# One layer's modulation sums, query projections and Fourier/gate stage in another order, with VectorE's order written out by hand

## The chip, the core and the metric

The kernel runs on one core of a Trainium2 chip. The core has five engines that work side by side, each through a queue of its own: TensorE (PE, matrix products, with a weight load of its own, PEld), VectorE (DVE), ScalarE (ACT), GpSimd (POOL) and SyncE (SP), which here only issues transfers between the chip's memory and SBUF. Matrix products end in PSUM, whose banks are read out by VectorE or ScalarE before they can be used again. The metric is the device time of one execution, in microseconds (us). The kernel before takes 1128.33 us, the median of three runs from 1126.88 to 1129.64.

## The reference

Two layers act on 1024 latent tokens of width 1024 with 256 context tokens. The work in question lies in layer 0. Cut to what matters:

```python
shift, scale, gate = split(silu(c) @ ada_w[i] + ada_b[i], 3)      # modulation, both layers
h  = rms_norm(x, norm_g) * (1 + scale) + shift                    # (1024, 1024)
hc = the same with c_ctx on the 256 context tokens
proj = h @ w_in                                                   # Fourier | q | k | v | gate
q = rope(rms_norm(q));  k, v = keys and values of context and latent tokens (1280)
o = softmax(q0 k0') v - lam * softmax(q1 k1') v                   # 4 heads of two halves
fo = fftn(u, axes=(tokens, channels of a group), norm="ortho").real   # 4 groups of 128 channels
y = concat([fo, rms_norm(o) * (1 - lam_init)]) * silu(gate part of proj)
x = x + gate * (y @ w_out)                                        # then layer 1, a short convolution
```

All is in float32. On TensorE a float32 product is made of three products of rounded parts: a value is split into `hi`, its rounding, and `lo`, the rest, and `hi*hi + lo*hi + hi*lo` is summed.

## The kernel before, in words

**Projections.** `proj_tok(tt, c)` makes a block of 128 tokens by 512 columns: eight pieces k of the inner dimension, three matmuls each (L284 to L286), 24 in all, into a PSUM bank. c=0 gives the keys, c=1 the values (tt = 0 to 9; the v stage), c=2 the queries (tt = 2 to 9; the query stage), c=3 the input of the Fourier mixer for eight blocks called m, in the order 0, 4, 2, 6, 1, 5, 3, 7, the first three made ahead. Inside a block, jobs are taken between the matmuls: at k = 4, 5 or 6 the transposes of an earlier key or query block (`qk_t`, L345 to L356: PE transposes into `ps_t`, ScalarE rounds to `th`, VectorE makes `tl`, both go to memory), and at k = 7 a column sum (`ada_c`, L583 to L587). Before its transpose a query block is normed and rotated (`qk_norm`, `qk_scaled`, `qk_a`): the square on ScalarE, the sum on VectorE, the power -1/2 on GpSimd (L310, L311), then five steps on VectorE to `od`. The transposes run three query blocks behind.

**Modulation sums.** Eight vectors of 512 (the gates of layer 0 and all six parts of layer 1) are made as sums: `ada_load` brings two pieces of 1 MB (`ada_raw`, three buffers of them), `ada_m` multiplies eight row blocks by the conditioning and adds them into `ada_sum`, four in a call (`half` 0 or 1). With `np_` = n the last n of the four are scaled by ScalarE (L573) and added by GpSimd (L574); the others are one VectorE instruction each (L576, L579). After the second half the sum is on a list, and `ada_step` makes a job of it, the column sum `ps_col`, which PE takes at k = 7 of the next block.

**Fourier and gate.** VectorE forms sums and differences of the eight input blocks (`fa`, `fe`, L691 to L698) and splits four results into the arena (`EO`, L706 to L708). For each of the four groups, `fft_a` multiplies the arena by cosines and sines (`ps_gc`, `ps_gs`), and `fft_b` multiplies that along the channels (`ps_fe`, `ps_fo`); `fee` and `mid` are copies out of PSUM. `gate_half(f, half)` makes 512 columns of the gate path directly, 24 matmuls into `ps_feat`. The other gate columns are made in three pairs g by a scheme of seven products instead of eight (`gate_product(g, p)`, p = 1 to 7), 12 matmuls each, into banks X, Y and Z of the pair (p = 6, 7, 4 use X after p = 1). Their left sides are hi and lo parts of `h` or of its sums: `t3` makes the difference for p = 3 and 7 in place, `tk` and `g_less` those for p = 5, 6 and 4, in `arena0`, `arena1` and `t4`. Their right sides come from `gop`, which combines weights on GpSimd and splits them on ScalarE (L61) and VectorE or GpSimd (L62). Of four pieces of each of these differences, one goes to GpSimd (`GE`). The results (`go`, `sg`) are copied or added out of the banks, and the attention follows, whose first head is loaded into the arena.

**What sets the order.** From the v stage on, PE runs in program order and the order on the other engines comes from a scheduler that works by cost estimates:

```python
    man = tc.manual_schedule(engines={ENG.PE})
    man.__enter__()
```

A buffer of a pool is free again when all readers of its last tile are done; a load into it, or an instruction that writes it, waits for that.

Of the kernel before, what the change touches and what calls it, by code (L numbers as in the profile page):

```python
# [37 lines left out]
def block_kernel(tc, A):  # L38
# [522 lines left out]
    def ada_m(half, np_=0):  # L561

        if half == 0 and adas:
            evs.append((*adas.pop(0), post.tile([P, NB], F32, name="ada_sum", tag="o", bufs=4), alds.pop()))
            if adas:
                alds.append(ada_load(*adas[0]))
# [22 lines left out]
    def ada_step(n):  # L589
        if n % 2 and sums:  # L590
            cols.append(lambda a=sums.pop(): ada_c(*a))
# [6 lines left out]
    for tt in range(NK):  # L598
# [6 lines left out]
        ada_m(tt % 2)  # L605
# [6 lines left out]
    for tt in range(NTC, NK):  # L612
# [4 lines left out]
        ada_step(tt)  # L617
        fins.append(qk_a(proj_tok(tt, 2, (5,)), 0, tt))
        ada_m(tt % 2, 2)
# [35 lines left out]
    ada_step(1)  # L655
    for m in (0, 4, 2):
        qk_b(*fins.pop(0))
        pf.append(proj_tok(NTC + m, 3, (5,)))
    assert not (adas or evs or sums or jobs or cols or fins)
    wnext(2)  # L660
    cls("post", "hc", "ada")

# [16 lines left out]
    fx = opn("fx", "right")  # L679


    for n in range(2):
        eo = []
        for m in (n, n + 2):
            psa = pf.pop(0) if pf else proj_tok(NTC + m, 3)
            a = fx.tile([P, NB], F32, name="fa", bufs=1)
            nc.scalar.copy(out=a, in_=psa)
            psb = pf.pop(0) if pf else proj_tok(NTC + m + 4, 3)
            for i, op in enumerate((ALU.add, ALU.subtract)):
                e = fx.tile([P, NB], F32, name=f"fe{i}", bufs=2)  # L690
                nc.vector.tensor_tensor(out=e, in0=a, in1=psb, op=op)  # L691
                eo.append(e)
        ea, oa, eb, ob = eo
# [12 lines left out]
        for (h, l), u in zip(EO, us):  # L706
            nc.scalar.copy(out=h[:, n, :], in_=u)
            nc.vector.tensor_sub(out=l[:, n, :], in0=u, in1=f32(h[:, n, :]))  # L708
    cls("fx")
# [35 lines left out]
    def fft_b(g, ch, cl, sh, sl, dh, dl):  # L745
# [4 lines left out]
        for pp, a, b, i, n in ((p6, dh, dl, 0, 2), (pe, ch, cl, 0, NB), (po, sh, sl, 2, NB)):  # L750
# [3 lines left out]
            if n == 2:  # L754
                nc.vector.tensor_copy(out=mid, in_=p6[:, 0:2])
        e = fev.tile([P, NB], F32, name="fee", bufs=1)
# [31 lines left out]
    def gate_half(f, half):  # L788
# [7 lines left out]
        gate_out(f, half, ge.tile([P, NB], F32, name="sg", bufs=2), ps)  # L796
# [15 lines left out]
    def gate_product(g, p):  # L812
# [6 lines left out]
        new = lambda: go.tile([P, NB], F32, name="go", bufs=5) if go else ge.tile([P, NB], F32, name="sg", bufs=2)  # L819
# [15 lines left out]
    tk = []  # L835

    def g_diff(t, k, a, b, eng):

        x, y = H[a][k[0]], H[b][k[1]]
        tt = lambda i, j, op: eng.tensor_tensor(out=t, in0=i, in1=f32(j), op=op)  # L840
        tt(f32(x[0]), y[0], ALU.subtract)
        tt(t, x[1], ALU.add)
        tt(t, y[1], ALU.subtract)

    def g_less(k, half, eng):
        x = H[half][k + 4]
        eng.tensor_tensor(out=tk[k], in0=f32(x[0]), in1=tk[k], op=ALU.subtract)
        eng.tensor_tensor(out=tk[k], in0=tk[k], in1=f32(x[1]), op=ALU.add)
# [5 lines left out]
    GE = (nc.vector, nc.vector, nc.vector, nc.gpsimd)  # L854
    def t3():
        for k in range(4):
            u = v0[:, hsl[k % 2]]
            g_diff(u, (k, k + 4), 1, 1, GE[k])
            nc.scalar.copy(out=H[1][k][0], in_=u)
# [774 lines left out]
```

## Time and profile before

| what | value |
|---|---|
| median of 3 runs | 1128.33 us (1126.88 to 1129.64) |
| profiled execution | 1128.21 us |
| its span, first to last instruction | 1126.4 us |
| mean granted clock of TensorE | 0.971 |
| PE busy | 1047.5 us (93%), 5118 matmuls |
| VectorE, GpSimd, ScalarE busy | 759.8, 497.8, 479.8 us |
| chain that ended last | PE 56%, VectorE 15%, ScalarE 4%, GpSimd 4% |

A row of the timeline gives the start in us, the duration, the engine, the line, the operation, the tile written and the tiles read, shape and type, and in brackets how long the engine was idle before and what ended it. A window row gives a stretch, its length, the engine's busy time and number of instructions, the granted clock, the share of the transfer engines and their rate.

### The profile page before, as it was taken

The page shows a single profiled execution, that of the slowest core. Times are in us where ns is not written, and L with a number is a line of the kernel's source. Part 1 is how long each engine was busy: PE and PEld are TensorE (multiplying, and loading weights), DVE is VectorE, ACT ScalarE, POOL GpSimd, SP SyncE. Part 2 cuts the span into 40 slices and gives each one's busy share as a digit, 9 for nine tenths or more (in the row PEclk, how much of TensorE's full clock was granted, in tenths as well). Part 3 has the DMA queues.
Part 4 walks back from the last instruction along what each step waited for, and adds up shares of the span by engine and source line. Part 5 has one row for each costly group of instructions (what it writes and reads, how often), then busy time and mean ns, then how long its engine had stood idle before and what let it go on. Part 6 is the DMA issues. An engine that isn't in the chain of part 4 may idle for free.

```text
span 1126.4 us, 14132 instructions
## 1 busy us (share of the span) xinstructions
PE 1047.5 (93%) x5118; PEld 854.1 (76%) x5118; DVE 759.8 (67%) x1073; ACT 479.8 (43%) x868; POOL 497.8 (44%) x422
## 2 busy tenths in 40 slices
PE   4989899979898989999999998989999999999898
PEld 2657688768786869899988886667888888787576
DVE  4599855883859368888883376996545645579842
ACT  4453213311334357777773363544333333343410
POOL 1256002740466325766666446473435343433331
PEclk9998899989898999999999999999999999999899
DMA  9724895533220596451102652022121211211421
GB/s 342 302 96 120 260 292 174 175 102 110 73 99 10 142 263 142 126 133 60 48 29 95 226 166 94 1 76 74 43 70 38 68 45 56 74 56 64 160 86 65
DMA packets 61381, 131.12 MB, mean 116 GB/s; under 512 B 5248, under 2 KB 30208, under 8 KB 58112
## 3 DMA queue, kind: packets, MB, share of 16 engines
q1 hardware_dynamic: 60240, 125.64, 35.6%
q0 software_dynamic: 1072, 4.59, 1.1%
q8 instruction: 40, 0.66, 0.3%
q14 instruction: 29, 0.24, 0.1%
HBM read 105.57 MB, written 24.64 MB: 116 GB/s over the span
## 4 chain that ended last, share of the span: by engine, by line
PE 56%; DVE 15%; ACT 4%; POOL 4%; issue 3%; DMA 0%; ACTq 0%; DVEq 0%; POOLq 0%
PE psX L649 6%; PE psX L650 6%; PE psX L651 6%; PE ps_av L1032 5%; PE psY L650 3%; PE psY L651 3%; PE psY L649 3%; PE S L982 3%; PE S L983 3%; PE ps_t L1022 2%; DVE nm L987 2%; PE ps_feat L1085 2%; PE ps_feat L1087 2%; PE ps_feat L1086 2%; PE psZ L651 1%
## 5 line engine op out<-in xcount | busy, mean ns | idle before, releaser
L61 ACT CAST wop<-wraw 128x512 fp32r<-128x512 f32 x152 | 93.2, 620 | 129.3 <-PE psY L651 28.4
L62 POOL TENSOR_TENSOR wop<-wraw,wop 128x512 fp32r<-128x512 f32 x72 | 100.7, 1402 | 71.2 <-ACT wop L61 71.2
L284 PE MATMUL ps_tok<-whi,hhi 128*128 128x512 f32 x288 | 120.8, 420 | 2.4 <-ACT hhi L393 2.4
L285 PE MATMUL ps_tok<-whi,hlo 128*128 128x512 f32 x288 | 117.6, 408 | 3.8 <-DVE hlo L397 3.8
L286 PE MATMUL ps_tok<-wlo,hhi 128*128 128x512 f32 x288 | 116.4, 404 | 0.0
L987 DVE TENSOR_REDUCE nm<-S 128x1 f32<-128x1280 f32 x64 | 95.0, 1487 | 21.7 <-PE S L983 18.7
L649 PE MATMUL psX<-B,wop 128*128 128x512 f32 x240 | 98.3, 410 | 11.6 <-DVE out L1363 3.4
L998 ACT ACTIVATE p<-S,nm 128x1280 f32<-128x1280 f32 x64 | 85.2, 1331 | 44.1 <-DVE nm L987 38.3
L650 PE MATMUL psX<-B,wop 128*128 128x512 f32 x240 | 97.8, 408 | 1.6 <-POOL B L1454 1.0
L651 PE MATMUL psX<-B,wop 128*128 128x512 f32 x240 | 97.3, 405 | 0.5 <-POOL wop L62 0.5
L628 POOL TENSOR_TENSOR s<-wraw 128x512 f32<-128x512 f32 x20 | 27.4, 1370 | 125.6 <-DMA wraw<-in_wodd_dram 118.5
L62 DVE TENSOR_TENSOR wop<-wraw,wop 128x512 fp32r<-128x512 f32 x80 | 65.6, 823 | 20.4 <-ACT wop L61 20.1
L1032 PE MATMUL ps_av<-v,aT 128*128 128x128 f32 x640 | 76.8, 275 | 0.0
L628 POOL TENSOR_TENSOR wraw<-wraw 128x512 f32<-128x512 f32 x40 | 56.4, 1420 | 43.0 <-DVE wop L62 35.5
L1032 PEld LDWEIGHTS ps_av<-v,aT 128*128 128x128 f32 x640 | 74.2, 192 | 0.2
L285 PEld LDWEIGHTS ps_tok<-whi,hlo 128*128 128x128 f32 x288 | 56.7, 197 | 18.8 <-DVE hlo L397 7.5
L284 PEld LDWEIGHTS ps_tok<-whi,hhi 128*128 128x128 f32 x288 | 56.7, 197 | 16.9 <-ACT hhi L393 3.7
L1009 POOL TENSOR_TENSOR p<-p,cc 128x256 f32<-128x256 f32 x32 | 40.3, 1261 | 65.2 <-DVE cc L1006 46.1
L649 PEld LDWEIGHTS psX<-B,wop 128*128 128x128 f32 x240 | 46.4, 193 | 26.8 <-issue 5.7
L650 PE MATMUL psY<-B,wop 128*128 128x512 f32 x160 | 63.8, 399 | 2.8 <-DVE B L1216 2.4
L286 PEld LDWEIGHTS ps_tok<-wlo,hhi 128*128 128x128 f32 x288 | 56.6, 197 | 12.3
L651 PE MATMUL psY<-B,wop 128*128 128x512 f32 x160 | 63.5, 397 | 1.5 <-DVE wop L62 1.5
(344 smaller groups left out, 2683.8 us busy)
## 6 DMA issues: line engine op xcount, KB each, us to landing
ada_raw<-in_ada_dram SPq DMA_DIRECT2D x24, 1024.0 KB, 6.8
wraw<-in_wodd_dram SPq DMA_DIRECT2D x32, 512.0 KB, 3.5
wraw<-in_wo_dram SPq DMA_DIRECT2D x24, 512.0 KB, 4.6
wraw<-in_wtok_dram SPq DMA_DIRECT2D x16, 512.0 KB, 5.0
arena<-kd SPq DMA_DIRECT2D x16, 320.0 KB, 8.8
kq<-kd SPq DMA_DIRECT2D x16, 320.0 KB, 9.8
xt<-in_xT_dram SPq DMA_DIRECT2D x16, 256.0 KB, 5.9
xr<-in_xT_dram SPq DMA_DIRECT2D x16, 256.0 KB, 4.0
```

What stands on the lines that cost most here:

```text
L61: nc.scalar.copy(out=o[:, 0, :], in_=src)
L62: eng.tensor_tensor(out=o[:, 1, :], in0=src, in1=f32(o[:, 0, :]), op=ALU.subtract)
L284: nc.tensor.matmul(ps, lhsT=hh, rhs=whi, start=k == 0, stop=False)
L285: nc.tensor.matmul(ps, lhsT=hl, rhs=whi, start=False, stop=False)
L286: nc.tensor.matmul(ps, lhsT=hh, rhs=wlo, start=False, stop=k == KT - 1)
L628: tt = lambda out, x, y, op: nc.gpsimd.tensor_tensor(out=out, in0=x, in1=y, op=op)
L649: nc.tensor.matmul(ps, lhsT=a, rhs=x[k][0], start=start and k == 0, stop=False, skip_group_check=not start)
L650: nc.tensor.matmul(ps, lhsT=a, rhs=x[k][1], start=False, stop=False, skip_group_check=not start)
L651: nc.tensor.matmul(ps, lhsT=b, rhs=x[k][0], start=False, stop=k == 3, skip_group_check=not start)
L987: nc.vector.tensor_reduce(out=nm, in_=S[m][:, :NKEY], op=ALU.max, axis=AX.X, negate=True)
L998: nc.scalar.activation(out=p, in_=S[m][:, :NKEY], func=AF.Exp, bias=tiles.pop((i, m, "nm")), accum_out=z)
L1032: nc.tensor.matmul(ps, lhsT=groups[i, k // 4][:, (k % 4) * P:(k % 4 + 1) * P], rhs=v[:, k * P:(k + 1) * P], start=k == 0, stop=k == NK - 1)
```

## The change

The sums. They are held in three kinds of buffers (`o`, `gt1_1`, `gt2_1`) instead of one. The v stage starts them at tt = 1 instead of 0, and takes half (tt+1)%2. A column sum is now only made a job while another sum is on the list (or no load is left), the oldest first, so that it comes a block pair later: the first four moved from blocks 3, 5, 7, 9 of the v stage to 5, 7, 9 and query block 4, the others from query blocks 3, 5, 7, 9 to 6, 8 and m = 0 and 2. In the query stage a half is wholly on ScalarE and GpSimd when tt is even, wholly on VectorE when it is odd; before, each half was shared two and two.

Fourier and gate. From there on VectorE, too, runs in program order. `tk` is formed early: two pieces between projections, two after the first half of the arena. All pieces that GpSimd had of `t3`, `tk` and `t4` go to VectorE. `t3` is in two parts around the first `fft_a`. Two gate halves stand before the first `fft_a`, and the rounding by ScalarE and the rest on VectorE are one step apart (`lagged`). `mid` is copied by ScalarE, `fee` lies in `v0`, `sg` has three buffers. The products come in another order, and a product's matmuls stand ahead of the next weight combination. The number of PE instructions is the same.

On PE, in the v stage (a piece of the difference; `ps_tok` is a projection, `ps_col` a column sum):

```order
 L285 MATMUL ps_tok<-whi,hlo 128x512
 L286 MATMUL ps_tok<-wlo,hhi 128x512
-L586 MATMUL ps_col<-ones,ada_sum 128x1 x4
 L284 MATMUL ps_tok<-whi,hhi 128x512
 L285 MATMUL ps_tok<-whi,hlo 128x512
```

The first column sum no longer stands in block 3; nothing takes its place there.

On GpSimd, in the second half of the query stage (`s` is the norm of a query block, one number behind it for each block). Before:

```order
L310 TENSOR_SCALAR s_1743<-s_1743 128x8
L574 TENSOR_TENSOR ada_sum<-ada_sum,ada_raw 128x512
L311 TENSOR_TENSOR s_1743<-s_1743,mhalf 128x8
L310 TENSOR_SCALAR s_1806<-s_1806 128x8
L311 TENSOR_TENSOR s_1806<-s_1806,mhalf 128x8
L574 TENSOR_TENSOR ada_sum<-ada_sum,ada_raw 128x512 x2
L310 TENSOR_SCALAR s_1862<-s_1862 128x8
L311 TENSOR_TENSOR s_1862<-s_1862,mhalf 128x8
L574 TENSOR_TENSOR ada_sum<-ada_sum,ada_raw 128x512 x2
```

And now:

```order
L310 TENSOR_SCALAR s_1789<-s_1789 128x8
L575 TENSOR_TENSOR ada_sum<-ada_sum,ada_raw 128x512
L311 TENSOR_TENSOR s_1789<-s_1789,mhalf 128x8
L575 TENSOR_TENSOR ada_sum<-ada_sum,ada_raw 128x512 x3
L310 TENSOR_SCALAR s_1852<-s_1852 128x8
L575 TENSOR_TENSOR ada_sum<-ada_sum,ada_raw 128x512
L311 TENSOR_TENSOR s_1852<-s_1852,mhalf 128x8
L575 TENSOR_TENSOR ada_sum<-ada_sum,ada_raw 128x512
L310 TENSOR_SCALAR s_1910<-s_1910 128x8
L311 TENSOR_TENSOR s_1910<-s_1910,mhalf 128x8
```

Four adds stand between two norms where two stood, and none behind the last norm.

On VectorE, between the last Fourier input block and the first FFT (`fe` are sums and differences of input blocks, `gop` gate weights, `arena` what the FFT reads, `v` a work tile). Before:

```order
L691 TENSOR_TENSOR fe_2244<-fa,ps_tok 128x512
L695 TENSOR_TENSOR v_2066<-fe_2186,fe_2242 128x512
L695 TENSOR_TENSOR v_2066<-fe_2188,fe_2244 128x512
L695 TENSOR_TENSOR fe_2186<-fe_2186,fe_2242 128x512
L62 TENSOR_TENSOR gop<-graw,gop 128x512
L695 TENSOR_TENSOR fe_2188<-fe_2188,fe_2244 128x512
L62 TENSOR_TENSOR gop<-s_2478,gop 128x512
L708 TENSOR_TENSOR arena_2064<-v_2066,arena_2064 128x512
L708 TENSOR_TENSOR arena_2065<-v_2066,arena_2065 128x512
L708 TENSOR_TENSOR arena_2064<-fe_2186,arena_2064 128x512
L62 TENSOR_TENSOR gop<-graw,gop 128x512
L708 TENSOR_TENSOR arena_2065<-fe_2188,arena_2065 128x512
```

And now:

```order
L708 TENSOR_TENSOR fe_2259<-v_2073,ps_tok 128x512
L708 TENSOR_TENSOR fe_2261<-v_2073,ps_tok 128x512
L715 TENSOR_TENSOR v_2073<-fe_2198,fe_2259 128x512
L715 TENSOR_TENSOR fe_2198<-fe_2198,fe_2259 128x512
L715 TENSOR_TENSOR v_2073<-fe_2200,fe_2261 128x512
L715 TENSOR_TENSOR fe_2200<-fe_2200,fe_2261 128x512
L728 TENSOR_TENSOR arena_2071<-v_2073,arena_2071 128x512
L728 TENSOR_TENSOR arena_2071<-fe_2198,arena_2071 128x512
L728 TENSOR_TENSOR arena_2072<-v_2073,arena_2072 128x512
L728 TENSOR_TENSOR arena_2072<-fe_2200,arena_2072 128x512
```

The three `gop` rows that stood among the arena's pieces are gone from there, and the arena comes in one piece (L728 is L708 of before).

The diff, cut to its core:

```diff
         if half == 0 and adas:
-            evs.append((*adas.pop(0), post.tile([P, NB], F32, name="ada_sum", tag="o", bufs=4), alds.pop()))
+            tag, n = (("o", 4), ("gt1_1", 1), ("gt2_1", 1))[len(adas) % 3 - 2]
+            evs.append((*adas.pop(0), post.tile([P, NB], F32, name="ada_sum", tag=tag, bufs=n), alds.pop()))
             if adas:
...
     def ada_step(n):
-        if n % 2 and sums:
-            cols.append(lambda a=sums.pop(): ada_c(*a))
+        if n % 2 and sums and (len(sums) > 1 or not adas):
+            cols.append(lambda a=sums.pop(0): ada_c(*a))
...
         ps = proj_tok(tt, 1, (4,))
-        ada_m(tt % 2)
+        if tt:
+            ada_m((tt + 1) % 2)
         v = post.tile([P, NB], F32, name="vo", tag="o", bufs=4)
...
             qk_b(*fins.pop(0))
-        ada_step(tt)
+        ada_step(tt + 1)
         fins.append(qk_a(proj_tok(tt, 2, (5,)), 0, tt))
-        ada_m(tt % 2, 2)
+        ada_m((tt + 1) % 2, 4 * (tt % 2 == 0))
     wnext(3)
...
     pf = []
-    ada_step(1)
     for m in (0, 4, 2):
         qk_b(*fins.pop(0))
+        ada_step((0, 4, 2).index(m) + 1)
         pf.append(proj_tok(NTC + m, 3, (5,)))
     cls("post", "hc", "ada")
+    man.__exit__(None, None, None)
+    man = tc.manual_schedule(engines={ENG.PE, ENG.DVE})
+    man.__enter__()
...
     fx = opn("fx", "right")
+    tk = []
+    for i in range(2):
+        tk += halves(wp.tile([P, T], F32, name="tk", tag="wraw", bufs=2))
+
+    def g_diff(t, k, a, b):
+
+        x, y = H[a][k[0]], H[b][k[1]]
+        tt = lambda i, j, op: nc.vector.tensor_tensor(out=t, in0=i, in1=f32(j), op=op)
+        tt(f32(x[0]), y[0], ALU.subtract)
+        tt(t, x[1], ALU.add)
+        tt(t, y[1], ALU.subtract)
+
             psa = pf.pop(0) if pf else proj_tok(NTC + m, 3)
-            a = fx.tile([P, NB], F32, name="fa", bufs=1)
+            a = v0[:, NB:T]
             nc.scalar.copy(out=a, in_=psa)
                 eo.append(e)
+            if m == 1:
+                g_diff(tk[2], (2, 2), 1, 0)
+                g_diff(tk[3], (3, 3), 1, 0)
         ea, oa, eb, ob = eo
...
             nc.vector.tensor_sub(out=l[:, n, :], in0=u, in1=f32(h[:, n, :]))
+        if n == 0:
+            g_diff(tk[0], (0, 0), 1, 0)
+            g_diff(tk[1], (1, 1), 1, 0)
     cls("fx")
...
             if n == 2:
-                nc.vector.tensor_copy(out=mid, in_=p6[:, 0:2])
-        e = fev.tile([P, NB], F32, name="fee", bufs=1)
+                nc.scalar.copy(out=mid, in_=p6[:, 0:2])
+        e = v0[:, 0:NB]
         nc.scalar.copy(out=e, in_=pe)
...
             nc.tensor.matmul(ps, lhsT=b, rhs=H[half][k][0], start=False, stop=k == KT - 1)
-        gate_out(f, half, ge.tile([P, NB], F32, name="sg", bufs=2), ps)
+        gate_out(f, half, ge.tile([P, NB], F32, name="sg", bufs=3), ps)
...
-    tk = []
-
-    def g_diff(t, k, a, b, eng):
-
-        x, y = H[a][k[0]], H[b][k[1]]
-        tt = lambda i, j, op: eng.tensor_tensor(out=t, in0=i, in1=f32(j), op=op)
-        tt(f32(x[0]), y[0], ALU.subtract)
-        tt(t, x[1], ALU.add)
-        tt(t, y[1], ALU.subtract)
-
-    def g_less(k, half, eng):
+    def g_less(k, half):
         x = H[half][k + 4]
-        eng.tensor_tensor(out=tk[k], in0=f32(x[0]), in1=tk[k], op=ALU.subtract)
-        eng.tensor_tensor(out=tk[k], in0=tk[k], in1=f32(x[1]), op=ALU.add)
+        nc.vector.tensor_tensor(out=tk[k], in0=f32(x[0]), in1=tk[k], op=ALU.subtract)
+        nc.vector.tensor_tensor(out=tk[k], in0=tk[k], in1=f32(x[1]), op=ALU.add)
     GB = {1: H[0][:4], 2: H[0][4:], 3: H[1][4:], 7: H[1][:4]}
-    GE = (nc.vector, nc.vector, nc.vector, nc.gpsimd)
-    def t3():
-        for k in range(4):
-            u = v0[:, hsl[k % 2]]
-            g_diff(u, (k, k + 4), 1, 1, GE[k])
-            nc.scalar.copy(out=H[1][k][0], in_=u)
-            GE[k].tensor_tensor(out=H[1][k][1], in0=u, in1=f32(H[1][k][0]), op=ALU.subtract)
+
+    def lagged(steps):
+
+        held = None
+        for a, b in steps:
+            r = a()
+            if held:
+                held()
+            held = lambda b=b, r=r: b(r)
+        held()
+
+    def rounded(src, hi):
+        nc.scalar.copy(out=hi, in_=src)
+
+    def rest(src, hi, lo):
+        nc.vector.tensor_tensor(out=lo, in0=src, in1=f32(hi), op=ALU.subtract)
+
+    def t3(ks):
+        def a(k):
+            u = ge.tile([P, NB], F32, name="s1", bufs=1) if k % 2 else v0[:, NB:T]
+            g_diff(u, (k, k + 4), 1, 1)
+            rounded(u, H[1][k][0])
+            return u
+
+        lagged([(lambda k=k: a(k), lambda u, k=k: rest(u, *H[1][k])) for k in ks])
+
+    def tpart(q, ks, half=None):
+
+        def a(k):
+            if half is not None:
+                g_less(k, half)
+            rounded(tk[k], q[k][:, 0, :])
+
+        lagged([(lambda k=k: a(k), lambda _, k=k: rest(tk[k], q[k][:, 0, :], q[k][:, 1, :])) for k in ks])
     gload(1)
-    for i in range(2):
-        tk += halves(wp.tile([P, T], F32, name="tk", tag="wraw", bufs=2))
-    for k in range(4):
-        g_diff(tk[k], (k, k), 1, 0, GE[k])
     gate_half(0, 1)
+    gate_half(1, 1)
+    t3((0, 1))
     cur = fft_a(0)
-    for g, fh in ((1, (1, 1)), (2, (0, 0)), (3, (1, 0))):
-        gate_half(*fh)
-        fft_b(*cur)
-        cur = fft_a(g)
-        if g == 1:
-            t3()
-            gop(0, 1)
-            gop(1, 1)
-            gop(0, 5)
+    t3((2, 3))
+    gate_half(0, 0)
+    gop(0, 1)
+    gop(1, 1)
+    fft_b(*cur)
+    cur = fft_a(1)
+    gate_half(1, 0)
+    gop(0, 5)
+    gop(0, 2)
+    fft_b(*cur)
+    cur = fft_a(2)
     gate_product(0, 1)
+    gop(1, 5)
+    fft_b(*cur)
+    cur = fft_a(3)
     gate_product(1, 1)
+    gop(1, 2)
+    qs = [quarter_of(t) for t in arena]
+    tpart(qs[0], range(4))
     fft_b(*cur)
     t4 = go.tile([P, 8 * NB], F32R, name="t4")
-    qs = [quarter_of(t) for t in (*arena, t4)]
-    GB.update({5: [(q[:, 0, :], q[:, 1, :]) for q in qs[0]], 6: [(q[:, 0, :], q[:, 1, :]) for q in qs[1]],
-               4: [(q[:, 0, :], q[:, 1, :]) for q in qs[2]]})
-    for k in range(4):
-        part(tk[k], qs[0][k], GE[k])
-    gop(0, 6)
-    for k in range(4):
-        g_less(k, 1, GE[k])
-        part(tk[k], qs[1][k], GE[k])
-    gop(0, 2)
-    gop(0, 7)
-    gop(1, 5)
-    for k in range(4):
-        g_less(k, 0, GE[k])
-        part(tk[k], qs[2][k], GE[k])
-    order = [(0, 5), (0, 6), (0, 2), (0, 7), (1, 5), (0, 4), (1, 6), (0, 3), (1, 7), (1, 2),
-             (2, 1), (1, 4), (2, 5), (2, 6), (1, 3), (2, 7), (2, 2), (2, 4), (2, 3)]
-    ahead = order[5:]
+    qs.append(quarter_of(t4))
+    for p, q in zip((5, 6, 4), qs):
+        GB[p] = [(t[:, 0, :], t[:, 1, :]) for t in q]
+    tpart(qs[1], range(4), 1)
+    order = [(0, 5), (0, 2), (1, 5), (1, 2), (0, 6), (1, 6), (0, 7), (1, 7), (0, 4), (0, 3), (1, 4), (1, 3),
+             (2, 1), (2, 5), (2, 6), (2, 2), (2, 7), (2, 4), (2, 3)]
+    ahead = order[4:]
     for n, (g, p) in enumerate(order):
+        gate_product(g, p)
+        if n in (2, 3):
+            tpart(qs[2], (2 * n - 4, 2 * n - 3), 0)
         if ahead:
                 gload(q[0] + 2)
-        gate_product(g, p)
     nc.scalar.activation(out=l2[:, 0:1], in_=last[0][:, 0:1], func=AF.Exp)
```

More of the change, by code (lines that the diff above doesn't have):

```diff
@@ L818, in gate_product @@
         f = 2 + 2 * g
-        new = lambda: go.tile([P, NB], F32, name="go", bufs=5) if go else ge.tile([P, NB], F32, name="sg", bufs=2)
+        new = lambda: go.tile([P, NB], F32, name="go", bufs=5) if go else ge.tile([P, NB], F32, name="sg", bufs=3)
         if p in (1, 6):
```

## The prediction

> **What bounds the kernel now.** I read the busy times first, then the waits of TensorE, then its timeline around each wait, and last the timelines of the engines named there.
>
> ```profile
> PE 1047.5 (93%) x5118; PEld 854.1 (76%) x5118; DVE 759.8 (67%) x1073; ACT 479.8 (43%) x868; POOL 497.8 (44%) x422
> ```
>
> TensorE (PE) is busy 93% of the span and each other engine 67% at most, so time goes where PE stops or runs slowly. Every wait of PE from 120 to 400 us (line waited at, what released it, us in total, times, longest):
>
> ```profile
> PE ps_col L586 <- POOL ada_sum L574: 8.0, 2, 6.7
> PE ps_col L586 <- DVE ada_sum L576: 4.7, 1, 4.7
> PE ps_gc L732 <- DVE arena L708: 3.9, 2, 3.5
> PE ps_fo L751 <- ACT fee L757: 3.3, 1, 3.3
> PE psX L649 <- ACT go L822: 2.2, 1, 2.2
> ```
>
> These 22.1 us lie at places that the diff touches. A stop costs more than its length, as PE's timeline shows (start, duration, instruction, what it waited for):
>
> ```profile
> 129.72 0.40 PE L286 MATMUL ps_tok<-wlo,hhi 128*128 128x512 f32 x1
> 134.79 1.84 PE L586 MATMUL ps_col<-ones,ada_sum 128*128 128x1 f32 x8 [4.68 <-DVE ada_sum L576]
> 142.80 0.60 PE L349 MATMUL ps_t<-cst,od 128*128 128x128 f32 x4
> ...
> 150.98 0.40 PE L286 MATMUL ps_tok<-wlo,hhi 128*128 128x512 f32 x1
> 152.02 0.48 PE L284 MATMUL ps_tok<-whi,hhi 128*128 128x512 f32 x1
> ...
> 212.80 0.40 PE L286 MATMUL ps_tok<-wlo,hhi 128*128 128x512 f32 x1
> 215.44 0.47 PE L284 MATMUL ps_tok<-whi,hhi 128*128 128x512 f32 x1
> ...
> 227.15 0.40 PE L286 MATMUL ps_tok<-wlo,hhi 128*128 128x512 f32 x1
> 242.75 0.60 PE L349 MATMUL ps_t<-cst,od 128*128 128x128 f32 x4
> 243.43 0.39 PE L285 MATMUL ps_tok<-whi,hlo 128*128 128x512 f32 x1
> 248.41 0.39 PE L286 MATMUL ps_tok<-wlo,hhi 128*128 128x512 f32 x1
> 248.64 0.60 PE L349 MATMUL ps_t<-cst,od 128*128 128x128 f32 x4
> ```
>
> Undisturbed, 22 matmuls lie between 243.43 and 248.41, so one takes 0.226 us; a block of 24 with its transposes takes 248.64 - 242.75 = 5.89; and a matmul with the column sum behind it takes 152.02 - 150.98 = 1.04, 0.09 more with the slower start after it. I call the five places A to F, with B and C for the two stops in the first row. A: 129.72 to 142.80 is 13.08 for a column sum and 15 matmuls, which need 1.04 + 0.09 + 15 x 0.226 = 4.52; lost 8.56. B: 215.44 - 212.80 - 1.04 = 1.60. C: 242.75 - 227.15 = 15.60, with 18 matmuls, so 15.60 - 1.13 - 4.07 = 10.40. What A and C lose beyond their stops (8.56 - 4.68 = 3.88 and 10.40 - 6.7 = 3.70) is the clock (window, busy, granted clock, DMA):
>
> ```profile
> 230.00:232.00 2.00, 0.00 (x0) 0.81 0.58 115
> 234.00:236.00 2.00, 1.74 (x9) 0.50 0.93 310
> 240.00:242.00 2.00, 2.00 (x7) 0.63 0.00 0
> ```
>
> It falls during the stop, and PE, back at work, is at half speed from 234 until about 241. The gate stage's three:
>
> ```profile
> 289.73 0.28 PE L730 MATMUL ps_gc<-tabs,arena 128*128 128x256 f32 x1
> 299.96 0.39 PE L793 MATMUL ps_feat<-hhi,whi 128*128 128x512 f32 x1
> 307.16 0.28 PE L730 MATMUL ps_gc<-tabs,arena 128*128 128x256 f32 x1
> 310.67 0.40 PE L793 MATMUL ps_feat<-hhi,whi 128*128 128x512 f32 x1
> ...
> 338.31 0.40 PE L753 MATMUL ps_fe<-gcl,cht 128*128 128x512 f32 x1
> 347.29 0.40 PE L649 MATMUL psY<-arena,gop 128*128 128x512 f32 x1
> ...
> 355.88 0.50 PE L649 MATMUL psX<-hhi,gop 128*128 128x512 f32 x1 [2.16 <-ACT go L822]
> ```
>
> D: the first fft_a takes 10.23, the second 3.51; lost 6.72. E: 338.31 to 347.29 is 8.98 for 13 matmuls, which need 13 x 0.226 + 0.09 = 3.03; lost 5.95. F: the stop itself, 2.16. A to C are 20.56, D to F 14.83, together 35.39, of which the slow clock is 3.88 + 3.70 + (6.72 - 3.92) + (5.95 - 3.30) = 13.0. The sum is made against the profiled execution, 1128.21 us, 0.12 below the median of 1128.33. With all six gone it would be 1092.8, which bounds the gain, since PE's work is the same.
>
> [...]
>
> **A to C, the modulation sums.** The eight sums keep their work; the column sums of the first four come two blocks later (first now in block 5 of the v stage), those of the last four later as well, the eighth in m=2 of the Fourier input instead of query block 9. A's sum had been released at 134.79; its new place is two blocks behind 129.72, at 129.72 + 2 x 24 x 0.226 = 140.6. Lead 5.8 us, cost 0. C's sum ended on GpSimd:
>
> ```profile
> 228.15 1.97 POOL L311 TENSOR_TENSOR s<-s,mhalf 128x8 f32<-128x8 f32 x1
> 230.55 3.65 POOL L574 TENSOR_TENSOR ada_sum<-ada_sum,ada_raw 128x512 f32<-128x512 f32 x2 [0.43 <-issue]
> ```
>
> It would now be read 3 x 5.89 = 17.7 us later. B likewise. So 20.56 us go, unless something that stood behind the adds becomes late. In the even query blocks all four adds are on GpSimd (4 x 3.65 / 2 = 7.3 us in a block of 5.89), none in the odd ones, so over two blocks with two norms (2.0 each) it has 11.3 us of work against 11.8: tight, but the transposes that need the norm run three blocks behind. Tighter is m=4, whose transpose waits for VectorE's `tl`, and this stands in VectorE's queue behind weight splits for which ScalarE first does the four scalings of the eighth sum:
>
> ```profile
> ada_raw<-in_ada_dram SPq DMA_DIRECT2D x24, 1024.0 KB, 6.8
> ...
> 215.16 1.34 ACT L573 ACTIVATE ada_raw<-ada_raw,cs 128x512 f32<-128x512 f32 x2 [6.56 <-DMA ada_raw<-in_ada_dram]
> 233.93 1.04 ACT L171 CAST whi<-wraw 128x1024 fp32r<-128x1024 f32 x1 [7.15 <-DMA wraw<-in_wg_dram]
> ...
> 235.13 1.22 DVE L172 TENSOR_TENSOR wlo<-wraw,whi 128x1024 fp32r<-128x1024 f32 x1
> 338.53 0.67 DVE L847 TENSOR_TENSOR tk<-hhi,tk 128x512 f32<-128x512 f32 x1
> ```
>
> The chain: load 6.8, scalings 2 x 1.34, casts 3 x 1.04, subtractions 3 x 1.22, a weight load (half the size of the sums' pieces, so above 3.4; estimated 4), `tl` 0.67: 20.9 us. In the order it starts 3.6 blocks ahead of PE's need, 21.2 us. Without lead, four hops that each wait for one instruction of 0.67 make it 2.7 late. Below: 0. Above: twice that with E's clock loss, 5.4 + 2.65 = 8.0. I take 2.7, the four hops.
>
> **D, the first FFT.** Two gate halves (48 x 0.226 = 10.8 us of PE) now stand ahead of it instead of one. VectorE has ten instructions of 0.67 between the eighth projection and the last arena piece, and no gate weights between them: 6.7 us plus one ScalarE cast of about 0.6, 7.3 against 10.8. D goes whole. If the cover is gone (the second gate half waits for its weights), D's 6.72 stays.
>
> **E, the odd half of fft_b.** It waited for the copy of `fee`, last in ScalarE's queue behind this:
>
> ```profile
> 339.84 0.62 ACT L61 CAST arena<-tk 128x512 fp32r<-128x512 f32 x1 [0.26 <-DVE tk L848]
> 341.36 0.59 ACT L757 COPY fee<-ps_fe 128x512 f32<-128x512 f32 x1
> ```
>
> Now the casts ahead of the last fft_b round `tk` that VectorE finished long ago, and what needs VectorE comes behind. ScalarE takes over the copy of `mid`, bounded by 0 and a full copy's 0.59; 0.4, nearer to the copy since the cost of starting stays. In the third fft_b the `fee` copy may stand behind a gate cast of 0.62: between 0 and 0.7, 0.35.
>
> **F, the product order.** The X bank alternates between groups, so the wait at 355.88 goes. Two costs: (0,6) comes fifth and needs the new arena1 pieces from VectorE, by my walk 0.7 early to 1.3 late, bounded 0 to 1.5, taken 0.75. And (2,7) to (2,4) share a bank back to back: PE waits for the matmul's drain, 0.17 more than its pitch (0.39 - 0.226), and a ScalarE copy, 0.59 as that of `fee`: 0.8. All that PE has left stands behind each of these two waits. VectorE takes 14 instructions from GpSimd, 12 pieces of `tk` move ahead of the first FFT; hidden while VectorE has idle time, and it has:
>
> ```profile
> 284.00:400.00 116.00, 75.87 (x94) 0.94 0.29 85
> 340.00:360.00 20.00, 19.63 (x21) 0.83 0.00 0
> ```
>
> 75.9 busy of 116, so 40.1 idle, though little of it in the second row. Price if the cover is gone: 14 x 0.67 = 9.4, at most 14 x 1.77 = 24.8 by this row beside GpSimd's work:
>
> ```profile
> 333.93 1.77 DVE L847 TENSOR_TENSOR tk<-hhi,tk 128x512 f32<-128x512 f32 x1
> ```
>
> **Sum.** 1128.21 - 35.39 + 2.7 + 0.4 + 0.35 + 0.75 + 0.8 = 1097.8, 1098 us.
>
> **The rivals.** First: the query stage stays late. The four adds in one piece push the norm or the weight splits past m=0 and m=4, with a stop at each and the halved clock. Priced between E (5.95) and C (10.40), 8.2 each, in place of the 2.7: 1097.8 - 2.7 + 16.4 = 1112. For it: 11.3 us of work in 11.8 on GpSimd. Against: three blocks of lead.
>
> Second: VectorE in program order is late at (0,6). Twelve VectorE instructions make the arena1 pieces, behind four for arena0; if half of the sixteen run at 1.77 instead of 0.67, (0,6) stops 8.8 us, with E's clock loss 2.65: 1097.8 + 11.4 = 1109. For it: 19.63 busy of 20 in 340 to 360. Against: four products (4 x 12 x 0.226 = 10.8 us) now stand ahead of it, and GpSimd has fewer instructions to disturb it. [...]
>
> Third: the sums' loads land late in the new buffers and A to C stay while D to F go: 1097.8 + 20.6 - 2.7 = 1116. For it: DMA is busy 0.93 at 234 to 236. Against: in program order a load moves by at most one block, its column sum by two or more.
>
> Fourth, slower: VectorE's idle time is no cover. In program order it waits at the head of its queue for PE's banks and ScalarE's casts, its 40.1 us stay idle as they were, and the 14 moved instructions come on top of the gate stage at 1.77: 1128.2 - 20.56 + 24.8 = 1132, D to F giving nothing. It is slower from 13 of the 14 exposed (23.0 against 20.56 + 2.3) and no change for 11 or 12. For it: an order by hand does not pass a waiting instruction. Against: the `tk` part lies where VectorE has only the Fourier sums to do.
>
> **How the numbers follow.** The likeliest 0.62 with 1098, its own range 1092.8 to 1092.8 + 8.0 + 0.6 + 0.7 + 1.5 + 0.8 = 1104; first 0.16, second 0.11, third 0.03, fourth 0.08 (half of it within 0.2%). A measurement tells 0.2%, 2.3 us, from no change. All but the fourth are faster: 0.92; same 0.04; slower 0.04. The range of 1092 to 1113 holds the likeliest and the first two, leaving out the third and fourth and the upper tails.
>
> **What would show it.** Right: no wait of `ps_col` for the sums, none of `ps_gc` for the arena, the granted clock at 1.00 from 126 us on, the Fourier input's last projection some 20 us earlier than 284. Wrong: a wait of `ps_t` or `ps_tok` over 3 us between 215 and 250 (first), a `psX` wait for arena at the fifth product (second), `ps_col` still waiting (third), VectorE over 90% busy through the gate stage with PE waiting for `gop` (fourth). A time over 1113 would mean that a new stop with its own halved clock has come.

## The result and the profile after

The changed kernel takes 1100.43 us (median of four runs, 1098.48 to 1103.36) against 1128.99 for the kernel before (four runs); the ratio is 0.9749, interval 0.9729 to 0.9769. Forecast were 1098 us and a range of 1092 to 1113. The profiled execution of the changed kernel is the slowest of its four, 1103.36 us with a span of 1101.6. TensorE's waits from 100 to 400 us (line waited at, what released it, us in total, times, longest):

```profile
...
PE ps_t L349 <- DVE tl L353: 2.3, 1, 2.3
PE psX L653 <- DVE gop L62: 2.2, 1, 2.2
...
PE psX L651 <- ACT go L852: 0.7, 1, 0.7
...
PE ps_fo L774 <- ACT mid L778: 0.3, 1, 0.3
PE ps_col L587 <- DVE tl L353: 0.2, 1, 0.2
```

None of the five waits of before is left: no `ps_col` for a sum, no `ps_gc` for the arena, no `ps_fo` for `fee`, and the two `psX` waits are others. The rows left out are the attention's. In the order of size the new ones are the transpose of m=4, the product (0,6), the reuse of the X bank by (2,4), and the copy of `mid`: the four places that the prediction named. TensorE's timeline around the first two (start, duration, instruction, in brackets the wait):

```profile
227.49 0.39 PE L286 MATMUL ps_tok<-wlo,hhi 128*128 128x512 f32 x1
230.20 1.11 PE L349 MATMUL ps_t<-cst,od 128*128 128x128 f32 x4 [2.32 <-DVE tl L353]
237.50 0.39 PE L286 MATMUL ps_tok<-wlo,hhi 128*128 128x512 f32 x1
...
328.46 0.40 PE L652 MATMUL psX<-arena,gop 128*128 128x512 f32 x1
331.07 0.50 PE L653 MATMUL psX<-arena,gop 128*128 128x512 f32 x1 [2.21 <-DVE gop L62]
335.97 0.40 PE L652 MATMUL psX<-arena,gop 128*128 128x512 f32 x1
```

From 227.49 to 237.50 is one block, 10.01 us instead of 5.89: 4.1 lost. From 328.46 to 335.97 there are 15 matmuls of 0.23, 3.45 us, in 7.51: 4.1 lost. About half of each is the clock (window, length, busy time and matmuls, granted clock, transfer share, rate):

```profile
230.00:231.00 1.00, 0.80 (x5) 0.58 0.62 180
...
233.00:234.00 1.00, 1.00 (x5) 0.71 0.82 229
...
332.00:333.00 1.00, 1.00 (x6) 0.78 0.00 0
...
335.00:336.00 1.00, 1.00 (x4) 0.51 0.62 238
```

The clock of a window tells when in it the speed changed: 0.58 is half speed for (1 - 0.58) x 2 = 0.84 us, so it fell at 230.16, as the stop ended (at 230.20). At the second place it fell at 332.56, 1.5 us after TensorE had gone back to work at 331.07.

The sum over the stages: 35.39 us of losses are gone, 4.1 + 4.1 + 0.7 + 0.3 = 9.2 are new, which makes 26.2. The first score product of the attention started at 401.18 and now starts at 375.76, 25.4 earlier, although this execution was 1.2 us late before the change begins (85.46 before, 86.68 after, the same instruction of the key stage), so 26.6 by the trace. The medians lie 28.6 apart; the other 2 us stand in no trace here. The two instructions, first before, then after:

```profile
85.46 0.79 PE L285 MATMUL ps_tok<-whi,hlo 128*128 128x512 f32 x1 [0.63 <-DVE hlo L397]
401.18 0.50 PE L982 MATMUL S<-arena 128*128 128x512 f32 x1 [0.78 <-DVE go L825]
```

```profile
86.68 0.50 PE L285 MATMUL ps_tok<-whi,hlo 128*128 128x512 f32 x1 [0.74 <-DVE hlo L397]
375.76 0.47 PE L1019 MATMUL S<-arena 128*128 128x512 f32 x1 [0.83 <-issue]
```

### The profile page after: what moved, and what is told of

The parts are those of the page before. It is cut to its first block, busy times and chain, and to the rows that moved or that the text cites. A ratio compares the mean times of both kernels' runs of the same rounds, so it can differ in the third digit from the quotient of the medians.

```text
span 1101.6 us, 14113 instructions
## 1 busy us (share of the span) xinstructions
PE 1037.6 (94%) x5118; PEld 846.6 (77%) x5118; DVE 756.2 (69%) x1079; ACT 481.7 (44%) x876; POOL 484.6 (44%) x412
## 4 chain that ended last, share of the span: by engine, by line
PE 64%; DVE 20%; POOL 5%; issue 5%; ACT 5%; DMA 0%; ACTq 0%; POOLq 0%; DVEq 0%
PE psX L651 6%; PE psX L653 6%; PE psX L652 6%; PE ps_av L1069 5%; PE ps_tok L284 3%; PE ps_tok L285 3%; PE ps_tok L286 3%; PE psY L652 3%; PE psY L653 3%; PE psY L651 3%; PE S L1019 3%; PE S L1020 3%; DVE nm L1024 2%; PE ps_t L1059 2%; PE ps_feat L1122 2%
## 5 line engine op out<-in xcount | busy, mean ns | idle before, releaser
L285 PE MATMUL ps_tok<-whi,hlo 128*128 128x512 f32 x288 | 115.2, 400 | 3.8 <-DVE hlo L397 3.8
```

The costliest lines, as they stand in the source:

```text
L285: nc.tensor.matmul(ps, lhsT=hl, rhs=whi, start=False, stop=False)
```

## The experiments

Theory: each of the losses A to F went at its own place, for the reason that the prediction gave, and the two stops that are left are VectorE's order. Rivals: the parts depend on each other; the gain comes from VectorE's program order as such; GpSimd is what matters. Ratios are against the kernel before, timed alongside.

| edit | median us | ratio, interval |
|---|---|---|
| the change | 1100.43 | 0.9749, 0.9729 to 0.9769 |
| e1 sums only | 1118.68 | 0.9905, 0.9869 to 0.9940 |
| e2 gate stage only | 1114.20 | 0.9870, 0.9833 to 0.9907 |
| e3 VectorE scheduled | 1101.54 | 0.9760, 0.9728 to 0.9791 |
| e4 one gate half ahead | 1099.24 | 0.9738, 0.9708 to 0.9768 |
| e5 weights of (0,6) ahead | 1098.75 | 0.9747, 0.9726 to 0.9768 |
| e6 eighth sum shared | 1100.70 | 0.9761, 0.9734 to 0.9788 |
| e7 all halves shared | 1101.57 | 0.9770, 0.9756 to 0.9785 |
| e8 e5 and e6 | 1099.38 | 0.9753, 0.9739 to 0.9767 |
| e9 late weight splits | 1098.36 | 0.9744, 0.9719 to 0.9768 |
| e10 e3 and e4 | 1100.27 | 0.9760, 0.9738 to 0.9782 |
| e11 a quarter on GpSimd | 1103.50 | 0.9791, 0.9766 to 0.9817 |
| e12 e9 and e5 | 1098.15 | 0.9737, 0.9714 to 0.9760 |

From e3 on the times lie within half a per cent of one another, and their intervals overlap, but for e11 and e12. What tells these apart is the trace, by the waits.

**e1: the sums alone.** The kernel before with this part of the diff:

```diff
-        ada_m(tt % 2)
+        if tt:
+            ada_m((tt + 1) % 2)
...
-        ada_m(tt % 2, 2)
+        ada_m((tt + 1) % 2, 4 * (tt % 2 == 0))
...
+        ada_step((0, 4, 2).index(m) + 1)
```

with the buffers and `ada_step` as in the change.

> The kernel before with the change of the modulation sums alone; Fourier and gate stage as before. Theory (the terms of the prediction add up, each at its place): A to C vanish (20.56 us) and the transpose of m=4 stops as in the changed kernel, where 227.49 to 237.50 took 10.01 us instead of 5.89, so 4.1 with its slow clock; gain 16.4, some 1112 us. D, E and F stay, with the waits of ps_gc, ps_fo and psX at 3.9, 3.3 and 2.2 us. Rival (the parts are tied: the scheduler's order of VectorE spoils the query stage without the program order behind it): ps_col or ps_t still waits over 4 us, gain under 10, over 1118 us.

The gain was 9.5 us (1128.14 to 1118.68), not 16.4. The rival held: `ps_t` waits 6.3 us. The sums no longer stop TensorE, and the waits of D, E and F are as before, but `ps_t` stops twice instead of once, and the first is longer. Waits, then VectorE's timeline:

```profile
PE ps_t L349 <- DVE tl L353: 3.4, 1, 3.4
PE ps_t L349 <- DVE od L340: 2.9, 1, 2.9
```

```profile
230.57 3.07 DVE L842 TENSOR_TENSOR tk<-tk,hlo 128x512 f32<-128x512 f32 x2
...
238.94 0.68 DVE L340 TENSOR_TENSOR od<-ko,kn 128x512 f32<-128x512 f32 x1
```

The scheduler, with VectorE free of order, draws the gate stage's `tk` into the query stage, ahead of the last `od`; two more of its pieces (1.28 us from 226.43) stand ahead of the late `tl`. In the change `tk` stands behind the Fourier sums by program order.

**e2: the gate stage alone.** The changed kernel with the sums as before (the edits of e1 reversed).

> The changed kernel with the modulation sums as before; Fourier and gate stage as changed. Theory: D to F (14.83 us) are gone, and the new stops of the changed kernel come in their place: 4.1 at (0,6) with its slow clock, 0.9 at (2,4), 0.3 in fft_b; net gain 9.5, some 1119 us, with ps_col waiting 4.7 and 8.0 us as before. Rival (the gate stage gains only because the sums are out of the way earlier): gain under 5, over 1123 us. Gains of this and of the sums alone should add up to the whole, 28.6.

Gain 13.9 us, more than the theory's 9.5 and near the whole of D to F. `ps_col` waits 4.5 and 8.5 us as before, (0,6) stops 2.2 again, up to 346.10, but in the profiled execution the clock did not fall after it (1.00 in every window of 1 us from 346 to 358). The gains of e1 and e2 sum to 23.4 against 28.6; by their intervals (6.8 to 14.8, and 10.5 to 18.8) the times do not refute that they add up, while the trace names what e1 alone pays: the stop of 2.9 us, half speed from 239.4 to 242.8 behind it, and a `tl` stop of 3.4 instead of 2.3. That E and F go with the gate stage's edits as a whole is shown here; which of these edits removes each was not tried.

**e3: VectorE's order from the scheduler.**

```diff
-    man = tc.manual_schedule(engines={ENG.PE, ENG.DVE})
+    man = tc.manual_schedule(engines={ENG.PE})
```

> The changed kernel with VectorE's order from the scheduler again, all else as changed. Theory (the gain of D to F comes from the cover ahead of the first FFT and from the product order, not from VectorE's program order): within 3 us of the changed kernel, 1098 to 1104; no ps_gc wait over 1 us although two gop rows again stand among the arena's. Rival (program order itself is what removes D and E): ps_gc or ps_fo waits over 2 us again and the time is 1105 to 1112.

The theory held: no wait of `ps_gc`, `mid` at 0.8, and (0,6) does not stop at all. It pays elsewhere: `ps_t` at m=4 now waits 3.4 for `tl`, with pieces of `tk` ahead of it in VectorE's queue, as in e1, and half speed from 229.2 to 236.0.

**e4: one gate half ahead.**

```diff
-    gate_half(1, 1)
-    t3((0, 1))
     cur = fft_a(0)
+    gate_half(1, 1)
+    t3((0, 1))
```

> The changed kernel with one gate half instead of two ahead of the first FFT, the other behind it, as it was before; VectorE in program order. Theory (the cover of D is the second gate half): in the changed kernel the last arena piece ended 7.9 us after the eighth projection, one gate half lasts 5.4, and the FFT's first pieces are needed at once, so ps_gc waits 1 to 2.5 us, with one slow stretch of the clock of 0 to 1.7: 1101 to 1105. Rival (the program order alone, without gop rows among the arena's, removes D): ps_gc waits under 0.5, within 1 us of the changed kernel.

The rival held: with half of the cover the FFT stops 0.2 us. The second gate half is not what removes D.

```profile
PE ps_gc L755 <- DVE arena L728: 0.2, 1, 0.2
```

**e10: both of these undone.** The edits of e3 and e4 together.

> The changed kernel with both undone: one gate half instead of two ahead of the first FFT, and VectorE's order from the scheduler. Either alone left no stop at the FFT. Theory (D's stop had two causes, each of which alone is enough to remove it: gop rows among the arena's pieces, and too little cover): with both back ps_gc waits 1.5 to 4 us and the time is 1102 to 1107. Rival (D went for another reason, such as GpSimd's weight combinations not disturbing VectorE there any more): ps_gc waits under 0.7, 1099 to 1102.

The rival held again: `ps_gc` waits 0.7, with one gate half ahead. Of the three gop rows that stood between VectorE's sums and pieces, only one is back (0.69 us at 274.44), so the old order is restored in part. What is left of D's cause is GpSimd. Its busy time and instructions from the eighth projection on, in the kernel before, and in the change:

```profile
284.00:300.00 16.00, 9.76 (x6) 0.79 0.25 92
```

```profile
268.00:284.00 16.00, 0.00 (x0) 1.00 0.27 91
```

VectorE ahead of the first arena piece in the kernel before, with one of the GpSimd instructions that ran beside it, and the same four VectorE instructions in e10:

```profile
286.38 2.38 DVE L695 TENSOR_TENSOR v<-fe,fe 128x512 f32<-128x512 f32 x2
288.29 1.62 POOL L628 TENSOR_TENSOR graw<-graw 128x512 f32<-128x512 f32 x1
288.69 1.77 DVE L695 TENSOR_TENSOR fe<-fe,fe 128x512 f32<-128x512 f32 x1
290.39 1.75 DVE L62 TENSOR_TENSOR gop<-graw,gop 128x512 fp32r<-128x512 f32 x1
```

```profile
271.60 1.29 DVE L715 TENSOR_TENSOR v<-fe,fe 128x512 f32<-128x512 f32 x2
272.81 0.68 DVE L715 TENSOR_TENSOR fe<-fe,fe 128x512 f32<-128x512 f32 x1
274.44 0.69 DVE L62 TENSOR_TENSOR gop<-graw,gop 128x512 fp32r<-128x512 f32 x1 [0.95 <-ACT gop L61]
```

Before, six instructions of weight combinations ran on GpSimd among the sums and arena pieces, and these four of VectorE took 5.90 us instead of 2.66: 3.2 more, against a stop of 3.5. In the change and in e10 the combinations come after the first FFT. What held them back there stands in the change's trace:

```profile
290.39 1.65 POOL L630 TENSOR_TENSOR s<-graw 128x512 f32<-128x512 f32 x1 [45.36 <-DVE hlo L882]
```

`hlo` is here the low part of the last piece of `t3`. The change gives every second piece of `t3` the buffer `s1`, of which there is one, and the first combination of `gop(0, 5)` writes into the same buffer; before, `t3` had none of it. In e10 that piece of `hlo` ends at 287.70 and the first combination starts at 287.78. In the kernel before, it started at 286.48, when its weights had landed, and likewise in e1 at 274.27, which has the old `t3` and keeps the whole of D. An edit that brings only the combinations back was not tried, so that they alone make D is argued from these rows and not shown.

**e5: the weights of (0,6) ahead.**

```diff
+    gop(0, 6)
     tpart(qs[1], range(4), 1)
...
-    ahead = order[4:]
+    ahead = order[5:]
...
-        if ahead:
+        if n and ahead:
```

> The changed kernel with the weights of product (0,6) combined and split ahead of the arena1 pieces instead of behind them. Theory (PE's 2.2 us at (0,6) are VectorE's order: the low part of these weights is its last instruction of that stretch, PE needs it at the third matmul, while the fourth arena1 piece is needed only 9 matmuls or 2.1 us after the first): the wait falls below 0.8 us, gain 1.5 to 2.2, and 1.7 more in runs whose clock fell: 1096 to 1099. Rival (VectorE has too much work before (0,6), whatever the order): the wait stays at 2 or above, now for arena1, and the time within 1 us of the changed kernel.

The theory held for the wait: 2.2 fell to 0.4, now for the arena. Another of 0.9 came behind it, so 0.9 net, and the median is 1.7 lower, which the intervals do not tell apart.

```profile
330.86 0.50 PE L652 MATMUL psX<-arena,gop 128*128 128x512 f32 x1 [0.40 <-DVE arena L882]
336.32 0.50 PE L651 MATMUL psX<-hhi,gop 128*128 128x512 f32 x1 [0.89 <-ACT go L845]
```

**e6: the eighth sum's second half shared, and e8: with e5.**

```diff
-        ada_m((tt + 1) % 2, 4 * (tt % 2 == 0))
+        ada_m((tt + 1) % 2, (2 if tt == 8 else 4) * (tt % 2 == 0))
```

> The changed kernel with the second half of the eighth sum shared two and two by GpSimd and VectorE instead of all four on ScalarE and GpSimd. Theory (the stop of ps_t at m=4 is the chain from the eighth sum's load over four scalings and the contended weight splits): ScalarE's casts come 1.2 us earlier and GpSimd disturbs less, against 1.4 us of adds on VectorE; the stop falls from 2.3 to 0.5 to 1.5, the time to 1097 to 1100. Rival (the stop is the weight load behind the first split, 5.3 us, and VectorE's own work, so the split of the sum does not matter): the stop stays at 2.0 to 3.5, the time at 1100 to 1102.

> The changed kernel with both edits, the weights of (0,6) ahead and the eighth sum's second half shared. Theory (the two stops that are left are independent): both waits below 1.5 us, no slow clock between 220 and 340 us, 1094 to 1097, and a smaller scatter between runs than the changed kernel's 4.9 us. Rival: one stop moves and the sum of both gains is not reached, 1098 to 1100.

The rivals held. In e6 the stop is 2.54, in e8 2.42: the scalings at the head of the chain do not set it. Of e8's theory the smaller scatter came, 1.3 us between its five runs against 4.9.

```profile
229.29 1.00 PE L349 MATMUL ps_t<-cst,od 128*128 128x128 f32 x4 [2.54 <-DVE tl L353]
```

**e7: every half shared as before.**

```diff
-        ada_m((tt + 1) % 2, 4 * (tt % 2 == 0))
+        ada_m((tt + 1) % 2, 2)
```

> The changed kernel with every half of the query stage shared two and two by VectorE and GpSimd, as before the change; later column sums, more buffers and the Fourier and gate stage as changed. Theory (the later column sums alone remove A to C; the split of halves by engine is not needed and costs the stop at m=4): no wait of ps_col over 0.5, the ps_t stop at most 1.5, 1097 to 1101. Rival (the split by engine is needed to have the sums in time): ps_col or ps_t waits over 3 us and the time is over 1104.

The theory held for the sums, which nowhere stop TensorE: A to C go without the split by engine. Later column sums and more buffers were not tried apart. The `tl` stop is gone, too, but `od` is late three times, by 4.0 in all against 2.3:

```profile
215.60 0.63 PE L349 MATMUL ps_t<-cst,od 128*128 128x128 f32 x4 [1.80 <-DVE od L340]
222.79 0.63 PE L349 MATMUL ps_t<-cst,od 128*128 128x128 f32 x4 [1.09 <-DVE od L340]
230.98 0.63 PE L349 MATMUL ps_t<-cst,od 128*128 128x128 f32 x4 [1.13 <-DVE od L340]
```

**e9: the last two weight splits late, and e12: with e5.** The call that makes them moves behind the first Fourier input sums:

```diff
-    wnext(2)
     cls("post", "hc", "ada")
...
+            if n == 0 and m == 0:
+                wnext(2)
+                for _ in range(2):
+                    tk += halves(wp.tile([P, T], F32, name="tk", tag="wraw", bufs=2))
```

> The changed kernel with the last two weight splits (gate weights, needed only at about 268 us) put behind the first Fourier input sums in VectorE's program order; ScalarE's casts of them stay where they were. Theory (the ps_t stop of 2.3 us is a queue matter: at 228.3 VectorE splits a weight that nobody needs yet and makes tl only behind it, at 229.5): tl comes 0.6 to 1.2 earlier, the stop falls to 1.1 to 1.7 and the rest is ScalarE's cast of the same weight, ahead of th. Rival (VectorE's share is nothing, th on ScalarE alone decides): the stop stays at 2.2 or more. The time is within 1.5 us of the changed kernel in both cases.

> The changed kernel with the last two weight splits late and the weights of (0,6) ahead of the arena1 pieces. Theory (both stops shrink independently): ps_t at most 1.7, (0,6) at most 0.5, 1096.5 to 1099, the fastest of these kernels by 1 to 3 us. Rival (what is left of the stops and the clock's chance outweigh it): 1099 to 1101, not told from the changed kernel.

The theories held for the waits. Of the times, e9's median is 2.1 lower than the changed kernel's (0.6 by the ratios), where at most 1.5 was expected, and e12 is ahead of e9 by 0.2, where 1 to 3 was. In the changed kernel the last weight piece landed at 227.2, ScalarE cast it ahead of `th`, and VectorE split it ahead of `tl` (ScalarE, then VectorE):

```profile
227.24 1.05 ACT L171 CAST whi<-wraw 128x1024 fp32r<-128x1024 f32 x1 [2.47 <-DMA wraw<-in_wg_dram]
228.19 0.58 ACT L351 CAST th<-ps_t 128x512 fp32r<-128x512 f32 x1
228.32 1.22 DVE L172 TENSOR_TENSOR wlo<-wraw,whi 128x1024 fp32r<-128x1024 f32 x1
229.47 0.68 DVE L353 TENSOR_TENSOR tl<-ps_t,th 128x512 fp32r<-128x512 f32 x1
```

These are gate weights, which TensorE first reads at 268. With the split out of the way, `tl` follows `th`, and the stop is 1.27 in e9 and 1.06 in e12, whose waits up to the attention are the shortest of all ((0,6) waits 0.40):

```profile
227.94 0.66 PE L349 MATMUL ps_t<-cst,od 128*128 128x128 f32 x4 [1.27 <-DVE tl L353]
```

```profile
227.87 0.66 PE L349 MATMUL ps_t<-cst,od 128*128 128x128 f32 x4 [1.06 <-DVE tl L353]
```

e12 is the fastest of these by its median, 1098.15, but its interval holds the changed kernel's ratio, so it is not shown to beat it. The rest of the stop would be ScalarE's cast ahead of `th`, 1.05 us in the rows above; this was not tried.

**e11: a quarter of the differences on GpSimd again.** `GE` as before the change, for the pieces k = 3:

```diff
+    GE = (nc.vector, nc.vector, nc.vector, nc.gpsimd)
...
-        nc.vector.tensor_tensor(out=tk[k], in0=f32(x[0]), in1=tk[k], op=ALU.subtract)
+        GE[k].tensor_tensor(out=tk[k], in0=f32(x[0]), in1=tk[k], op=ALU.subtract)
```

and in `g_diff` and `rest` alike.

> The changed kernel with a quarter of the differences (the pieces k = 3 of t3, tk and t4) on GpSimd again, as before the change. Theory (the move of these instructions to VectorE is worth little either way: VectorE gets 0.6 us back for each, but GpSimd's instructions slow others from 0.67 to 1.77): the time is within 1.5 us of the changed kernel, the wait at (0,6) 1 to 3 us. Rival (GpSimd's pieces at 1.3 to 1.8 us each, behind its weight work, come last): the wait at (0,6) grows to 4 or more with the slow clock, 1104 to 1109.

The theory was wrong about the size: (0,6) waits 3.9 instead of 2.2, with the slow clock behind it (a mean of 0.57 from 332 to 336), and the median is 3.1 us higher, both just short of the rival's bounds. VectorE has fewer instructions before (0,6) and ends later, since more of the others run beside GpSimd:

```profile
PE psX L653 <- DVE gop L62: 3.9, 1, 3.9
```

```profile
326.46 3.46 DVE L884 TENSOR_TENSOR arena<-tk,arena 128x512 fp32r<-128x512 f32 x2
329.34 1.71 POOL L62 TENSOR_TENSOR gop<-graw,gop 128x512 fp32r<-128x512 f32 x1
329.85 1.75 DVE L62 TENSOR_TENSOR gop<-graw,gop 128x512 fp32r<-128x512 f32 x1
```

The intervals of e11 and of the change overlap (from 0.9766 and up to 0.9769), so the 3 us are likely rather than certain; the wait is measured.

## Why the prediction was right

The likeliest case came, 2.4 us above its number and inside its own range of 1092.8 to 1104. The places were right; D went by luck, and two prices were too small. By its steps:

- **A to C** went whole, 20.56 us, and for the reason given: the column sums stand later. e7 shows that one engine for a half is not needed for it; the buffers were not tried apart.
- **The transpose at m=4**: priced 2.7 (bounds 0 and 8.0), measured 4.1, of which 2.3 is the stop. The place and the queue were right, the head of the chain was not: e6 took two scalings out and the stop stayed. The split of a weight ahead of `tl` is 1.05 of the 2.3 (e9); the rest, that weight's load and cast ahead of `th`, is read from rows. The term was too small by the clock, which stood only in its upper bound.
- **D** went whole, but the step gave the wrong cover, so this term was right by luck. It named the second gate half, and the gop rows that stood between. e4 takes the gate half away, e10 brings one of the rows back as well, and the FFT waits 0.2 and 0.7. The 6.7 us of VectorE's work were right for undisturbed instructions; that GpSimd's combinations leave that stretch, held back by the buffer `s1`, was not in the working.
- **E** went; the wait for the copy of `mid` is 0.28 for 0.4, and the third fft_b waits for nothing, for 0.35. The reason given, the order of casts, was not tried apart.
- **F** went; (2,4) cost 0.73 for 0.8. (0,6) was priced 0.75 between 0 and 1.5 and stopped 2.2, 4.1 with the clock: outside its bounds, the step that was most in error. Its walk ended at the arena1 pieces and took VectorE's instructions at 0.67; of those before (0,6) three ran at 1.67 to 1.78 beside GpSimd's gop work, as in the two rows below, and what TensorE waited for was the weights' low part behind them. The second rival priced such instructions at 8.8 us; they came at a quarter of that. With e5 the order alone brings the wait to 0.4.

```profile
324.23 1.83 POOL L62 TENSOR_TENSOR gop<-graw,gop 128x512 fp32r<-128x512 f32 x1 [1.80 <-ACT gop L61]
324.82 1.78 DVE L882 TENSOR_TENSOR arena<-tk,arena 128x512 fp32r<-128x512 f32 x1
```

- **The moved instructions**: hidden, as said. e11 shows more, that they are better on VectorE.
- **The first rival** (the norm or the weight splits late behind the adds) came at one of its two places, m=4, by a weight split, at 4.1 for 16.4. Its norm shows in e7, where VectorE is idle 2.19 us for it ahead of the first of the three stops; ahead of the other two stand weight splits of 1.2. The third and the fourth have no trace: no `ps_col` waits for a sum, and D to F did give their gain.
- **The signs**: the Fourier input's last projection starts its last matmul at 268.10 instead of 284.05, 16 us earlier and not 20, since the stop at m=4 took 4.1. The granted clock was not at 1.00 throughout, as it fell to 0.50 at 230.16 and at 332.56, with both stops.

The two misses have one sign, 1.4 and 3.3 us, and 3.4 of these 4.7 are the two stretches at half speed, each of which costs half of its 3.42 us, behind stops that the sum had at full clock.

## What to carry to other kernels

Read first what each stop costs from the starts on both sides of it, clock included; that sum bounds the gain, and it held here. To price an instruction of VectorE, look at what GpSimd does beside it in the new order: 0.67 and 1.77 us are the same instruction. When an engine is late at a place, ask what in its queue is not yet needed by anyone; moving that back (e9), or what is needed first ahead (e5), shortened the waits, and taking work out of the head of the late chain did not (e6). When a stop goes, look for what else the edit moved: here a shared buffer seems to have done what the cover was credited with.

## What the runs showed of the hardware

The clock's fall is not a matter of the stop's length alone. A stop of 2.3 us was followed by half speed in the change, one of 2.2 was not in e4, and one of 3.45 was not in e1 (stop from 227.25 to 230.70), where the windows show full clock throughout:

```profile
227.00:231.00 4.00, 0.55 (x5) 1.00 0.23 66
231.00:239.00 8.00, 5.83 (x28) 1.00 0.24 68
```

```profile
226.00:230.00 4.00, 1.79 (x11) 1.00 0.23 67
230.00:234.00 4.00, 4.00 (x19) 1.00 0.70 200
```

(the first e1, the second e4). Between 100 and 400 us of both kernels' traces the stretches at half speed have three lengths only. In the change 0.84 + 2 + 0.58 = 3.42 us by its windows, and 3.42 again at (0,6); at D and E, by windows of 1 us, 292.68 to 299.52 and 340.46 to 347.30, twice that; in the kernel before, C lasts (1 - 0.62) x 2 = 0.76, then 9, then (1 - 0.76) x 2 = 0.48, together 10.2, three times as long:

```profile
231.00:232.00 1.00, 0.00 (x0) 0.62 0.59 176
232.00:241.00 9.00, 6.74 (x20) 0.50 0.47 149
241.00:242.00 1.00, 1.00 (x5) 0.76 0.00 0
```

So the clock fell at 231.24 in C, while TensorE stood (idle until 234.26), and in the change once as the stop ended and once 1.5 us later. The stops of 2.3 and 2.2 us in the change went with 3.42 us at half speed each, D's 3.5 and E's 3.3 with 6.84, C's 6.7 with 10.2, and e1's 3.45 with none. A stop has cost none, one, two or three of the shortest stretches here, and what decides between these was not shown.

At half speed each 3.42 us cost 1.71. For a new stop with a slow clock the prediction had 2.65, which is what E lost beyond its stop.

That the falls of the clock are also the cause of the 4.9 us between the changed kernel's runs is likely and was not shown, since only one execution of each kernel was profiled. The mean granted clock of the fastest run, 0.989 against 0.981 and 0.982 for the other three, fits in sign.
